# A SwiGLU down projection as seven block products over 1024 tokens

## The chip, the cores and the metric

The kernel runs on one core of one Trainium2 chip. The metric is the device time of one execution in microseconds; before the change the median of three runs is 2809.4 us. All operands are fp32 in HBM, and the result is too.

## The reference

One layer of a decoder trunk over 2048 tokens of width 1024 (D_FF is 2816). The part that matters is the channel sub-layer at the end and the norm after it:

```python
h = h + g1 * mix
u = rmsnorm(h, norm2_w[l]) * (1.0 + sc2) + sh2
ff = (jax.nn.silu(u @ w_ffn_gate[l]) * (u @ w_ffn_up[l])) @ w_ffn_down[l]
h = h + g2 * ff
return rmsnorm(h, final_norm_w)
```

Ahead of it stand the adaLN vectors, one input projection, four HGRN2 heads, four differential attention heads and the output projection.

## The kernel before

**Precision.** TensorE multiplies in a rounded fp32 form. Each operand is therefore split into a high part (a cast on ScalarE, L114) and a low part (the operand less its high part, on VectorE, L115), and each product is three matmuls: high by high, low by high, high by low. A matmul here has 128 stationary columns and 512 moving ones.

**Stages.** In the profiled execution: adaLN and the input projection until about 400 us, attention and HGRN2 until 1131, output projection and second norm until 1420, gate and up for the later 1024 tokens until 1842, their down projection until about 2100, gate and up for the earlier 1024 tokens until 2552, their down projection to the end. The later tokens (s=1, blocks 3 and 2) come before the earlier (s=0, blocks 1 and 0); a block is 512 tokens.

**Gate and up** (`activations`, `seven`, L954 to L1030). For each of 11 values of p two feature blocks of 128 are computed for 1024 tokens. Each such product is a 2 by 2 block product by seven products in place of eight (Strassen's method, in the form with 15 sums). `combine` makes the sums of u2, the input, ahead (`x`, `y`, `w`, `t1` to `t4`, each a high and a low tile, L855 to L928); `seven` makes the sums of the weights (`s1` to `s4`, L967 to L971) in two tiles of the tag wsum. Its seven products have 12 matmuls each. `up` multiplies the two results and stores them to `act_d` (L1027), one store of 256 KB for each feature block and token block.

**Down projection** (`down`, L1048 to L1114), once for each block of 512 tokens. It runs over 22 feature blocks f. A step loads the activations of f (256 KB, into a `slot`) and the row block of `w_down` (512 KB, into a `wraw`), splits both (`sh`, `sl`, `wh`, `wl`, four buffers each) and issues 24 matmuls: four token tiles, two column halves, three products (L1079). All eight PSUM banks hold one block's result. The last steps are held back and issued token tile by token tile (2 steps for s=1, 4 for s=0), so that a tile's scaling can begin while the next is multiplied. At f == 8 gate, norm weight and residual `h_d` are loaded (L1063 to L1069). At the end each tile is scaled by `g2` (L1106), added to the residual (L1108, L1111), normed (L1089 to L1098) and stored (L1099).

**What sets the order.** The program is written in one order, and a list scheduler then orders the instructions of each engine's queue by its own model of their times. Each engine works through its queue in order. Loads stand in SP's queue, most stores in POOL's. Beside the down projections of s=1 run `make_u2` for the earlier tokens and the parts of `combine(0)` (`first`, `second` in block 2; `third`, `fourth` behind it), handed to `down` as `others` and taken one a step.

Of the kernel before, what the change touches and what calls it, by code (L numbers as in the profile page):

```python
# [14 lines left out]
ALU = mybir.AluOpType  # L15
# [26 lines left out]
NRAW, NW, NTMP = 3, 4, 8  # L42
# [6 lines left out]
def kernel(ctx: ExitStack, tc: tile.TileContext, io: dict, out: bass.AP):  # L49
# [61 lines left out]
    act_d = [[dram.tile([P, TB], F32, name=f"actd{b}_{f}") for f in range(NF)] for b in range(NTB)]  # L111
# [718 lines left out]
    pu7 = ctx.enter_context(tc.tile_pool(name="pu7", bufs=1))  # L830
    pt5 = ctx.enter_context(tc.tile_pool(name="pt5", bufs=1))
    later.close()
    ps = ctx.enter_context(tc.tile_pool(name="ps", bufs=1, side="right"))
# [16 lines left out]
    def combine(s):  # L850
# [20 lines left out]
        def first():  # L871
            for kk in range(4):
                x, z = load(kk, 0, 0), load(kk, 0, 1)
                put("x", kk, x)
                DVE.tensor_tensor(x, z, x, op=ALU.subtract)
                w = load(kk, 1, 1)
                DVE.tensor_tensor(x, w, x, op=ALU.subtract)
                put("t2", kk, x)
                DVE.tensor_tensor(w, w, z, op=ALU.subtract)
                put("t3", kk, w)  # L880
                yield

        def second():
            for kk in range(4):
                put("y", kk, load(kk, 1, 0))
# [3 lines left out]
                yield  # L889

        def third():
            for kk in range(4):
                put("w", kk, load(kk, 1, 1))
                yield

        def fourth():
            for kk in range(4):
                x, z = load(kk, 0, 0), load(kk, 0, 1)
                DVE.tensor_tensor(x, z, x, op=ALU.subtract)
                w, y = load(kk, 1, 1), load(kk, 1, 0)  # L900
                DVE.tensor_tensor(x, w, x, op=ALU.subtract)
                DVE.tensor_tensor(x, y, x, op=ALU.subtract)
                put("t4", kk, x)
                yield

        def together():

            kept = []
            for kk in range(4):
# [3 lines left out]
                t2 = ps.tile([P, TB], F32, name="t2", tag="sh", bufs=4)  # L913
# [16 lines left out]
        return made, first(), second(), third(), fourth(), together()  # L930

    def big(name, tag, bufs, dt=F32):
        return (ps if tag == "wsum" else pf).tile([P, D], dt, name=name, tag=tag, bufs=bufs)
# [11 lines left out]
    def split_small(src):  # L945
        h = ps.tile([P, TB], F32R, name="sh", tag="sh", bufs=4)
        lo = ps.tile([P, TB], F32R, name="sl", tag="sl", bufs=4)
# [6 lines left out]
    def seven(src, f0, u, finish):  # L954
# [4 lines left out]
            load_big(src[:, (f0 + j) * P:(f0 + j + 1) * P].rearrange("(k p) c -> p k c", p=P), NK)  # L959
            for j in range(2)  # L960
# [51 lines left out]

    def activations(s, u):

        for p in range(NP):
# [7 lines left out]

            def up(j, t, ps, sb):
                a = sl[j, t]
                DVE.tensor_tensor(a, sb if ps is None else ps, a, op=ALU.mult)  # L1026
                POOL.dma_start(out=act_d[2 * s + t][2 * p + j], in_=a)  # L1027

            seven(w_gate, 2 * p, u, gate)
            seven(w_up, 2 * p, u, up)  # L1030

    def single(take):

        left = []

        def one():
            if not left:
                left.extend(take())
            return left.pop(0)
        return one  # L1040

    def down_step(b, f, at):

        t = at()
        SP.dma_start(out=t, in_=act_d[b][f])
        return f, split_small(t), split_big(load_big(w_down[f * P:(f + 1) * P, None, :], 1))

    def down(b, at, first, others=(), after=()):  # L1048
# [4 lines left out]
        tags = (("acc", 2), ("acc", 2), ("sc", 2), ("sc", 2), ("hg", 2), ("hg", 2), ("pv", 1), ("tr", 1))  # L1053
        pds = [bank(*t) for t in tags]
        place = slots([f"u{z}{k}" for z in "hl" for k in range(4)])
        ho = [place() for tt in range(NT)]
        place = slots(T4[4:])
        fw, g2 = place(), place()
        ws = []
        for f in range(NF):  # L1060
            ws.append(first.pop(0) if first else down_step(b, f, at))
            next(others, None)
            if f == 8:  # L1063
                for c in range(2):
                    cs = slice(c * TB, (c + 1) * TB)
                    SP.dma_start(out=g2[c], in_=gate_d[1][:, cs])
                    SP.dma_start(out=fw[c], in_=bcast_row(io["final_norm_w"][cs]))
                    for tt in range(NT):
                        SP.dma_start(out=ho[tt][c], in_=h_d[b][tt * P:(tt + 1) * P, cs])  # L1069

            if NF - (LAST if b else LAST0) <= f < NF - 1:
                continue
            for tt in range(NT):
                tsl = slice(tt * P, (tt + 1) * P)
                for cc in ((0,), (1,)) if not b and f == NF - 1 else ((0, 1),):
                    for g, a, w in ws:
                        for m, (x, y) in enumerate(((0, 0), (0, 1), (1, 0))):
                            for c in cc:
                                PE.matmul(  # L1079
                                    pds[2 * tt + c], a[x][:, tsl], w[y][:, c * TB:(c + 1) * TB],  # L1080
# [105 lines left out]
```

## Time and profile before

| | |
|---|---|
| median of 3 runs | 2809.4 us (2808.2 to 2815.19) |
| the profiled execution | 2806.66 us |
| its span | 2804.8 us |
| mean granted TensorE clock | 0.988 of full speed |
| TensorE busy | 2706.7 us, 97% |
| VectorE busy | 1709.4 us, 61% |
| ScalarE busy | 1124.3 us, 40% |
| GpSimd busy | 327.4 us, 12% |
| moved over the span | 403.52 MB, 144 GB/s |

Times of engines are busy times of one profiled execution. They overlap, so they don't add up to the span. TensorE's matmuls are pipelined, with ends that are modelled: a busy TensorE may still be waiting inside. The span runs from the first to the last instruction that the profile shows; the time of the execution is a little longer. In the rows, PE is TensorE, PEld its weight loads, DVE VectorE, ACT ScalarE, POOL GpSimd, SP SyncE, and L1079 is line 1079 of the kernel before.

### The profile page before, as it was taken

To read this page: it belongs to the slowest core of one execution; us is meant where nothing else is said; L and a number is where in the kernel's file an instruction comes from. 1 tells how busy PE (TensorE), PEld (TensorE's weight loads), DVE (VectorE), ACT (ScalarE), POOL (GpSimd) and SP (SyncE) were. 2 spreads that over 40 slices of the span, in tenths; PEclk is the share of its full clock that TensorE was granted. 3 is DMA by queue.
4 is the path that set the end of the run, shared out by engine and by line. 5 is a ranking of instruction groups with operands and counts; after the bars stand their busy time and mean duration, and the time that the engine had idled before them with its cause. 6 is when DMAs were issued, how large, how long until landed. Compare 5 with 4: busy or idle time off the path is not lost.

```text
span 2804.8 us, 40363 instructions
## 1 busy us (share of the span) xinstructions
PE 2706.7 (97%) x15017; PEld 2320.0 (83%) x15017; DVE 1709.4 (61%) x3456; ACT 1124.3 (40%) x2062; POOL 327.4 (12%) x493
## 2 busy tenths in 40 slices
PE   6999999999999998898999999999999999999998
PEld 5888879999999997897878888878887888888886
DVE  6434557777777779664585555553757555554354
ACT  4542135565565666543342222242433222222232
POOL 2552200000010000112210000020101000000010
PEclk9999999999999999998999999999999999999999
DMA  8765672434234220656542222274845222226461
GB/s 274 262 210 171 215 224 79 136 121 132 80 117 143 72 91 31 220 178 224 171 129 89 76 75 83 83 281 150 299 132 162 86 75 79 79 83 221 140 217 61
DMA packets 306104, 403.52 MB, mean 144 GB/s; under 512 B 22970, under 2 KB 208620, under 8 KB 305780
## 3 DMA queue, kind: packets, MB, share of 16 engines
q1 hardware_dynamic: 276788, 307.60, 34.4%
q0 software_dynamic: 29120, 93.35, 9.0%
q8 instruction: 118, 1.93, 0.3%
q14 instruction: 78, 0.64, 0.1%
HBM read 309.63 MB, written 91.23 MB: 143 GB/s over the span
## 4 chain that ended last, share of the span: by engine, by line
PE 74%; DMA 4%; DVE 4%; issue 3%; ACT 1%; POOL 1%; SPq 0%; POOLq 0%; DVEq 0%; ACTq 0%
PE ps_sc L985 8%; PE ps_hg L985 8%; PE ps_acc L985 8%; PE ps_acc L174 8%; PE ps_acc L162 5%; PE ps_acc L1079 4%; PE ps_sc L1079 4%; PE ps_hg L1079 4%; PE ps_pv L633 4%; PE ps_pv L1079 2%; PE ps_tr L985 2%; PE ps_pv L985 2%; PE ps_tr L1079 2%; PE ps_tr L629 2%; PE ps_sc L603 2%
## 5 line engine op out<-in xcount | busy, mean ns | idle before, releaser
L115 DVE TENSOR_TENSOR wl<-wraw,wh 128x1024 fp32r<-128x1024 f32 x252 | 307.5, 1221 | 98.4 <-ACT wh L114 94.9
L114 ACT CAST wh<-wraw 128x1024 fp32r<-128x1024 f32 x252 | 263.6, 1047 | 221.3 <-PE ps_acc L174 111.5
L174 PE MATMUL ps_acc<-wh,uh 128*128 128x256 f32 x1040 | 295.5, 286 | 0.8 <-ACT uh L505 0.6
L174 PE MATMUL ps_acc<-wl,uh 128*128 128x256 f32 x1040 | 293.8, 284 | 2.1 <-DVE wl L115 2.1
L174 PE MATMUL ps_acc<-wh,ul 128*128 128x256 f32 x1040 | 292.3, 284 | 0.0
L114 ACT CAST wh<-wsum 128x1024 fp32r<-128x1024 f32 x88 | 92.3, 1049 | 307.5 <-issue 142.7
L174 PEld LDWEIGHTS ps_acc<-wl,uh 128*128 128x128 f32 x1040 | 196.0, 189 | 4.9 <-DVE wl L115 2.3
L174 PEld LDWEIGHTS ps_acc<-wh,uh 128*128 128x128 f32 x1040 | 195.7, 189 | 3.8 <-ACT uh L505 1.4
L174 PEld LDWEIGHTS ps_acc<-wh,ul 128*128 128x128 f32 x1040 | 194.9, 189 | 2.3 <-issue 0.2
L115 DVE TENSOR_TENSOR sl<-slot,sh 128x512 fp32r<-128x512 f32 x88 | 60.5, 690 | 203.3 <-ACT sh L114 200.0
L612 ACT ACTIVATE s<-s,mx 128x2048 f32<-128x2048 f32 (+15 forms) x128 | 154.0, 1203 | 47.0 <-DVE mx L607 45.3
L607 DVE CUSTOM_DVE_ANT_0 s<-ps_sc,dist,mx 128x512 f32<-128x512 f32 x192 | 143.5, 748 | 44.1 <-PE ps_sc L604 39.6
L114 ACT CAST sh<-slot 128x512 fp32r<-128x512 f32 x88 | 54.2, 620 | 259.2 <-PE ps_tr L1079 217.5
L633 PE MATMUL ps_pv<-vt,wt 128*128 128x128 f32 x1088 | 150.8, 278 | 3.3 <-ACT wt L631 3.1
L633 PEld LDWEIGHTS ps_pv<-vt,wt 128*128 128x128 f32 x1088 | 140.4, 194 | 11.0 <-ACT wt L631 5.9
L115 DVE TENSOR_TENSOR wl<-wsum,wh 128x1024 fp32r<-128x1024 f32 x88 | 107.5, 1222 | 68.7 <-ACT wh L114 65.7
L162 PE MATMUL ps_acc<-ul,wh 128*128 128x512 f32 x352 | 141.9, 404 | 1.0 <-DMA ul<-ud 1.0
L162 PE MATMUL ps_acc<-uh,wh 128*128 128x512 f32 x352 | 142.1, 406 | 0.0
L1027 POOL DMA_DIRECT2D actd<-t x88 | 47.9, 544 | 798.1 <-DVE t L1026 793.8
L162 PE MATMUL ps_acc<-uh,wl 128*128 128x512 f32 x352 | 140.3, 400 | 0.4 <-DVE wl L115 0.4
L985 PE MATMUL ps_hg<-cuh,wh 128*128 128x512 f32 x352 | 139.6, 397 | 0.0
L985 PE MATMUL ps_hg<-cul,wh 128*128 128x512 f32 x352 | 139.5, 396 | 0.0
(406 smaller groups left out, 7028.1 us busy)
## 6 DMA issues: line engine op xcount, KB each, us to landing
wraw<-in_w_in_dram SPq DMA_DIRECT2D x88, 512.0 KB, 4.2
wraw<-in_w_ffn_down_dram SPq DMA_DIRECT2D x88, 512.0 KB, 3.7
wraw<-in_w_ffn_gate_dram SPq DMA_DIRECT2D x44, 512.0 KB, 3.9
wraw<-in_w_ffn_up_dram SPq DMA_DIRECT2D x44, 512.0 KB
actd<-t POOLq DMA_DIRECT2D x88, 256.0 KB, 2.5
slot<-actd SPq DMA_DIRECT2D x88, 256.0 KB, 5.0
ada_w<-in_w_ada_dram SPq DMA_DIRECT2D x64, 256.0 KB, 3.9
wraw<-in_w_out_dram SPq DMA_DIRECT2D x32, 512.0 KB, 4.2
```

Of the source, the lines that this page charges most:

```text
L114: ACT.copy(dst_h, src)
L115: DVE.tensor_tensor(dst_l, src, dst_h.bitcast(F32), op=ALU.subtract)
L162: PE.matmul(pa, a[:, k % 4, j * P:(j + 1) * P], c, start=n == 0, stop=n == 3 * NK - 1)
L174: PE.matmul(pa[:, j], a[:, tt * P:(tt + 1) * P], c[:, k % 4], start=n == 0, stop=n == 3 * NK - 1)
L603: PE.matmul(ps[:, :n], qs[m][0][:, qc], ks[m][pc][:, :n], start=True, stop=False)
L607: DVE.tensor_tensor_reduce(out=s[:, lo:hi], in0=ps[:, :hi - lo], in1=dist[:, u0_:u0_ + hi - lo], op0=ALU.add, op1=ALU.min, scale=-slope, s ...
L612: ACT.activation(s[:, :W], s[:, :W], AF.Exp, scale=-1.0, bias=mx[:, npiece - 1:npiece], accum_out=mx[:, 4:5])
L629: PE.transpose(out=pt[:, j - g], in_=S[0][:, j * P:(j + 1) * P], identity=ident)
L633: PE.matmul(pv[:, :P], wt[:, j - g], vq[j // 4][:, j % 4], start=j == 0, stop=j == i)
L985: PE.matmul(pa[:, cs], a, c[:, cs], start=first and i == 0, stop=i == 11 and cs.stop == TB, skip_group_check=not first)
L1027: POOL.dma_start(out=act_d[2 * s + t][2 * p + j], in_=a)
L1079: PE.matmul(pds[2 * tt + c], a[x][:, tsl], w[y][:, c * TB:(c + 1) * TB], start=g == 0 and m == 0, stop=g == NF - 1 and m == 2,)
```

## The change

The down projection, too, is made by seven products. `down(s)` now covers 1024 tokens at once: two token blocks by two halves of D_FF against two halves of D_FF by two halves of the columns. Each of the seven products runs over 11 values of k; a step has 12 matmuls (four token tiles, three products, 512 columns), and there are 77 steps for each s. Products 0 to 6 use two sets of four PSUM banks in turn; products 2 and 6 add to what the product before left in their set (`start` stays false).

- `activations` now makes feature blocks p and p + 11 in one group. `up` makes the four operand sums (L1050 to L1060) as the results come and stores seven tensors where it stored four (L1036).
- `weights(k)` makes the four sums of `w_down`'s blocks (L1017 to L1020), in the first of the two gate and up stages alone, between gate and up of each group, and stores them to `wd_d`.
- `down_load` loads two steps in a pair: two raw tiles of the tag wraw2 (NRAW is now 4), each filled by two loads of 256 KB, and each split as one tile of 128x1024 into `wh2` and `wl2` (four buffers, thus two pairs).
- `finished` combines a product's result when it is complete: `c2` and `c3` hold the shared partial results, `result` scales by `g2` (L1120) and adds to the residual (L1122). `g2` is now in one of the two wsum buffers, `fw` in g1's tile; the residual of all eight token tiles is loaded at step 11.
- `combine` has the parts `most` (taken every second step, from the ninth on, within `down(1)`) and `rest` (behind it); `first` to `fourth` go. The norms of s=1 come behind its down projection, those of the later half of s=0 at the start of product 6.

```diff
-NRAW, NW, NTMP = 3, 4, 8
+NRAW, NW, NTMP = 4, 4, 8
...
-        lo = ps.tile([P, TB], F32R, name="sl", tag="sl", bufs=4)
+        lo = ss.tile([P, TB], F32R, name="sl", tag="sh", bufs=4)
...
+    def weights(k):
+
+        r1, r2 = (load_big(w_down[f * P:(f + 1) * P, None, :], 1) for f in (k, k + NP))
+        b11, b12 = r1[:, :TB], r1[:, TB:]
+        b21, b22 = r2[:, :TB], r2[:, TB:]
+        DVE.tensor_tensor(b22, b22, b12, op=ALU.subtract)
+        DVE.tensor_tensor(b12, b12, b11, op=ALU.subtract)
+        DVE.tensor_tensor(b11, b22, b11, op=ALU.add)
+        DVE.tensor_tensor(b21, b11, b21, op=ALU.subtract)
+        for n, t in ((1, b11), (3, b22), (4, b12), (5, b21)):
+            POOL.dma_start(out=wd_d[n][k], in_=t)
...
+                elif (j, t) == (0, 1):
+                    s1, s2 = other(), other()
+                    DVE.tensor_tensor(s1, a, sl[1, 1], op=ALU.add)
+                    store(4, s1)
+                    DVE.tensor_tensor(s2, s1, sl[0, 0], op=ALU.subtract)
+                    store(1, s2)
+                    DVE.tensor_tensor(a, sl[0, 0], a, op=ALU.subtract)
+                    store(3, a)
+                    sl["s2"] = s2
...
+            fs = (p, p + NP)
+            seven(w_gate, fs, u, gate)
+            if s:
+                weights(p)
+            seven(w_up, fs, u, up)
...
+                SP.dma_start(out=raw[:, z * TB:(z + 1) * TB], in_=src)
+            if i + 1 < NS:
+                ops.append(split_big(raw))
...
+        def finished(n, tt):
+
+            pa = sets[n % 2][tt]
+            if n == 0:
+                ACT.copy(c2[tt], pa)
+            elif n == 1:
+                DVE.tensor_tensor(c2[tt], c2[tt], pa, op=ALU.add)
+            elif n == 2:
+                result(0, 0, tt, pa)
+            elif n == 3:
+                DVE.tensor_tensor(c3[tt], c2[tt], pa, op=ALU.add)
+            elif n == 4:
+                result(1, 1, tt, pa, ALU.add, c3[tt])
+
+                DVE.tensor_tensor(c2[tt], c2[tt], g2[:, TB:], op=ALU.mult)
+                DVE.tensor_tensor(ho[0][tt][1], ho[0][tt][1], c2[tt], op=ALU.add)
+            elif n == 5:
+                result(1, 0, tt, pa, ALU.subtract, c3[tt])
+            else:
+                result(0, 1, tt, pa)
...
+                for g, (a, w) in held:
+                    kk = g % NP
+                    for m, (x, y) in enumerate(((0, 0), (0, 1), (1, 0))):
+                        PE.matmul(
+                            sets[n % 2][tt], a[x][:, tt * P:(tt + 1) * P], w[y],
+                            start=kk == 0 and m == 0 and n not in (2, 6), stop=kk == NP - 1 and m == 2,
+                            skip_group_check=n in (2, 6),
+                        )
+                if k == NP - 1:
+                    finished(n, tt)
...
+    steps = down_load(1, 0) + down_load(1, 2)
+    _, norms = down(1, steps, itertools.chain([None] * 8, most))
+    run(calls(*norms), rest)
     activations(0, made)
+    steps = down_load(0, 0) + down_load(0, 2)
+    down(0, steps)
```

Lines in the rows that follow are those of each kernel's own text. L1079 is the old down projection's matmul and L1189 the new one's; L115 and L123 are the subtraction of a split.

**First place: the middle of a down projection.** TensorE's queue before, most of one step of 24 matmuls (`sh`, `sl` the activations, `wh`, `wl` the weights):

```order
L1079 MATMUL ps_acc<-wh_19347,sh 128x512 x2
L1079 MATMUL ps_acc<-wl_19348,sh 128x512 x2
L1079 MATMUL ps_acc<-wh_19347,sl 128x512 x2
L1079 MATMUL ps_sc<-wh_19347,sh 128x512 x2
L1079 MATMUL ps_sc<-wl_19348,sh 128x512 x2
L1079 MATMUL ps_sc<-wh_19347,sl 128x512 x2
L1079 MATMUL ps_hg<-wh_19347,sh 128x512 x2
L1079 MATMUL ps_hg<-wl_19348,sh 128x512 x2
L1079 MATMUL ps_hg<-wh_19347,sl 128x512 x2
```

TensorE's queue now, the first step of a pair (the first operand named is the weights' part, the second the activations'):

```order
L1189 MATMUL ps_hg<-wh_20071,wh_20064 128x512 x2
L1189 MATMUL ps_pv<-wh_20071,wh_20064 128x512
L1189 MATMUL ps_tr<-wh_20071,wh_20064 128x512
L1189 MATMUL ps_hg<-wl_20072,wh_20064 128x512
L1189 MATMUL ps_hg<-wh_20071,wl_20065 128x512
L1189 MATMUL ps_hg<-wl_20072,wh_20064 128x512
L1189 MATMUL ps_hg<-wh_20071,wl_20065 128x512
L1189 MATMUL ps_pv<-wl_20072,wh_20064 128x512
L1189 MATMUL ps_pv<-wh_20071,wl_20065 128x512
L1189 MATMUL ps_tr<-wl_20072,wh_20064 128x512
L1189 MATMUL ps_tr<-wh_20071,wl_20065 128x512
```

VectorE's queue now, at the end of product 2 (`t` a temporary, `g` the gate, `slot` the residual):

```order
L123 TENSOR_TENSOR wl_20011<-wraw_20007,wh_20010 128x1024
L123 TENSOR_TENSOR wl_20018<-wraw_20014,wh_20017 128x1024
L1120 TENSOR_TENSOR t_19963<-ps_acc,g_19252 128x512
L1120 TENSOR_TENSOR t_19969<-ps_acc,g_19252 128x512
L1120 TENSOR_TENSOR t_19975<-ps_sc,g_19252 128x512
L1120 TENSOR_TENSOR t_19981<-ps_sc,g_19252 128x512
L1122 TENSOR_TENSOR slot<-slot,t_19963 128x512
L1122 TENSOR_TENSOR slot<-slot,t_19969 128x512
L1122 TENSOR_TENSOR slot<-slot,t_19975 128x512
L1122 TENSOR_TENSOR slot<-slot,t_19981 128x512
L123 TENSOR_TENSOR wl_20065<-wraw_20061,wh_20064 128x1024
L123 TENSOR_TENSOR wl_20072<-wraw_20068,wh_20071 128x1024
```

On TensorE the four high by high matmuls of a pair's first step have moved to the front. On VectorE eight passes of `result` stand between one pair's two subtractions and the next pair's. Where `most` runs beside the loop, ten passes of `combine` stand in one row ahead of a pair's first subtraction, and three between it and the second.

**Second place: the handover from the down projection of s=1 to the next gate and up stage.** VectorE's queue before (`wsum` the sums of the first groups' weights):

```order
L115 TENSOR_TENSOR wl_20656<-wraw_20653,wh_20655 128x1024
L971 TENSOR_TENSOR wsum<-wraw_20867,wsum 128x512
L115 TENSOR_TENSOR sl<-wraw_20869,sh 128x512
L115 TENSOR_TENSOR wl_20872<-wraw_20867,wh_20871 128x1024
L115 TENSOR_TENSOR sl<-wraw_20998,sh 128x512
L115 TENSOR_TENSOR wl_20880<-wsum,wh_20879 128x1024
L1106 TENSOR_TENSOR t_20707<-ps_acc,slot 128x512
L967 TENSOR_TENSOR wsum<-wraw_20998 128x512
L1106 TENSOR_TENSOR t_20708<-ps_acc,slot 128x512
L1111 TENSOR_TENSOR slot<-slot,t_20707 128x512
L968 TENSOR_TENSOR wsum<-wsum,wraw_20996 128x512
L1111 TENSOR_TENSOR slot<-slot,t_20708 128x512
```

VectorE's queue now, from the first scaling of product 6 on:

```order
L1120 TENSOR_TENSOR t_20887<-ps_acc,g_19252 128x512
L1120 TENSOR_TENSOR t_20896<-ps_acc,g_19252 128x512
L123 TENSOR_TENSOR wl_21094<-wsum,wh_21093 128x1024
L1120 TENSOR_TENSOR t_20905<-ps_sc,g_19252 128x512
L123 TENSOR_TENSOR sl<-wraw_21212,sh 128x512
L1120 TENSOR_TENSOR t_20914<-ps_sc,g_19252 128x512
L1122 TENSOR_TENSOR slot<-slot,t_20887 128x512
L1122 TENSOR_TENSOR slot<-slot,t_20896 128x512
L1122 TENSOR_TENSOR slot<-slot,t_20905 128x512
L901 TENSOR_TENSOR t_21021<-t_21023,t_21021 128x512
L1122 TENSOR_TENSOR slot<-slot,t_20914 128x512
L969 TENSOR_TENSOR wsum<-wraw_21081,wraw_21083 128x512
```

The sums of the first group's weights stood ahead of the last scalings (the last of them, L971, five rows above the first L1106); now two of the four, L969 and L970, stand behind eleven rows that begin with product 6's scaling.

**Third place: the end.** VectorE's queue before, the last rows of the program:

```order
L1106 TENSOR_TENSOR t_25519<-ps_pv,slot 128x512
L1108 TENSOR_TENSOR slot<-slot,t_25519 128x512
L1094 TENSOR_TENSOR f_r<-fss 128x1
L1095 TENSOR_SCALAR f_r<-f_r 128x1
L1098 SCALAR_TENSOR_TENSOR slot<-slot,f_r 128x512 x2
L1106 TENSOR_TENSOR t_25520<-ps_tr,slot 128x512
L1108 TENSOR_TENSOR slot<-slot,t_25520 128x512
L1094 TENSOR_TENSOR f_r<-fss 128x1
L1095 TENSOR_SCALAR f_r<-f_r 128x1
L1098 SCALAR_TENSOR_TENSOR slot<-slot,f_r 128x512 x2
```

VectorE's queue now, from the last product's first scaling on (an L1131 for each lot, an L1132 and a second row of four L1136 follow):

```order
L1120 TENSOR_TENSOR t_25664<-ps_acc,g_24123 128x512
L1120 TENSOR_TENSOR t_25692<-ps_acc,g_24123 128x512
L1122 TENSOR_TENSOR slot<-slot,t_25664 128x512
L1120 TENSOR_TENSOR t_25720<-ps_sc,g_24123 128x512
L1120 TENSOR_TENSOR t_25748<-ps_sc,g_24123 128x512
L1122 TENSOR_TENSOR slot<-slot,t_25692 128x512
L1122 TENSOR_TENSOR slot<-slot,t_25720 128x512
L1131 TENSOR_TENSOR f_r<-fss 128x1
L1122 TENSOR_TENSOR slot<-slot,t_25748 128x512
L1131 TENSOR_TENSOR f_r<-fss 128x1
L1132 TENSOR_SCALAR f_r<-f_r 128x1 x2
L1136 SCALAR_TENSOR_TENSOR slot<-slot,f_r,fw 128x512 x4
```

Before, one token tile's row (L1098, two of them) stood behind the last column half. Now the scalings of four token tiles and the two rows of L1136 for them stand behind the last product.

## Rows read from the trace of the kernel before

**Rows 1.** The page's head: the span, and each engine's busy time, share and instructions.

```profile
span 2804.8 us, 40363 instructions
...
PE 2706.7 (97%) x15017; PEld 2320.0 (83%) x15017; DVE 1709.4 (61%) x3456; ACT 1124.3 (40%) x2062; POOL 327.4 (12%) x493
```

**Rows 2.** The page's chain that ended last: shares of the span by engine.

```profile
PE 74%; DMA 4%; DVE 4%; issue 3%; ACT 1%; POOL 1%; SPq 0%; POOLq 0%; DVEq 0%; ACTq 0%
```

**Rows 3.** Busy time by stretch: PE, PEld, DVE, ACT, POOL, PEclk, DMA share, GB/s.

```profile
1420.00:1842.00 422.00, 420.54 (x1810) 338.57 (x1811) 247.43 (x338) 124.78 (x174) 24.32 (x45) 0.99 0.28 89
1852.00:2092.00 240.00, 238.54 (x1048) 193.47 (x1047) 129.78 (x182) 89.16 (x133) 21.34 (x33) 0.99 0.62 213
2092.00:2140.00 48.00, 43.74 (x179) 33.49 (x177) 39.97 (x68) 17.39 (x33) 9.64 (x12) 0.96 0.65 208
...
2566.00:2792.00 226.00, 224.86 (x968) 181.97 (x966) 99.93 (x133) 68.75 (x104) 10.15 (x15) 1.00 0.44 143
```

**Rows 4.** The chain in order of time: start, us, twelve matmuls of a step.

```profile
2785.27 2.80 PE ps_pv L1079 x12
```

**Rows 5.** Groups by line, 1842 to 2092: busy us, mean ns; idle before, releasers.

```profile
L115 DVE TENSOR_TENSOR wl<-wraw,wh 128x1024 fp32r<-128x1024 f32 x43 | 52.6, 1223 | 9.3 <-ACT wh L114 9.2
L114 ACT CAST wh<-wraw 128x1024 fp32r<-128x1024 f32 x43 | 45.0, 1046 | 3.3 <-DMA wraw<-in_w_ffn_down_dram 3.3
L115 DVE TENSOR_TENSOR sl<-slot,sh 128x512 fp32r<-128x512 f32 x44 | 30.2, 689 | 80.1 <-ACT sh L114 76.9 <-PE ps_pv L1079 3.2
L114 ACT CAST sh<-slot 128x512 fp32r<-128x512 f32 x44 | 27.1, 619 | 108.5 <-PE ps_tr L1079 80.2 <-issue 24.7 <-PE ps_pv L1079 3.6
...
L199 DVE TENSOR_SCALAR slot<-slot,u_r 128x512 f32<-128x512 f32 x16 | 6.9, 480 | 1.2 <-POOL u_r L197 0.9 <-DMA slot<-actd 0.4
L535 DVE TENSOR_SCALAR t<-ps_pv,a,modc 128x512 f32<-128x512 f32 x8 | 6.5, 809 | 12.6 <-PE ps_pv L207 12.6
...
L1098 DVE SCALAR_TENSOR_TENSOR slot<-slot,f_r 128x512 f32<-128x512 f32 x8 | 5.6, 745 | 0.0
...
L1111 DVE TENSOR_TENSOR slot<-slot,t 128x512 f32<-128x512 f32 x8 | 5.3, 685 | 0.0
```

**Rows 6.** Timeline, middle of a down projection: start, us, instruction [idle before it].

```profile
1966.46 0.62 ACT L114 CAST sh<-slot 128x512 fp32r<-128x512 f32 x1 [4.02 <-PE ps_tr L1079]
...
1968.07 1.23 DVE L115 TENSOR_TENSOR wl<-wraw,wh 128x1024 fp32r<-128x1024 f32 x1 [0.25 <-ACT wh L114]
```

**Rows 7.** Timeline of a gate and up group: two of VectorE's passes.

```profile
1608.53 0.68 DVE L970 TENSOR_TENSOR wsum<-wraw,wraw 128x512 f32<-128x512 f32 x1
...
1609.13 0.68 DVE L971 TENSOR_TENSOR wsum<-wraw,wsum 128x512 f32<-128x512 f32 x1
```

**Rows 8.** DMA, 1990 to 2040, then 1852 to 2092: KB, us to landing.

```profile
DMA packets 7762, 17.70 MB, mean 354 GB/s; under 512 B 913, under 2 KB 913, under 8 KB 7758
...
slot<-hd SPq DMA_DIRECT2D x12, 256.0 KB, 7.6
```

**Rows 9.** TensorE's waits, 2088 to 2145: us, times, longest; a stretch as above.

```profile
PE ps_sc L985 <- DVE wl L115: 2.6, 1, 2.6
...
2132.00:2136.00 4.00, 3.82 (x13) 2.53 (x12) 3.84 (x7) 0.59 (x1) 0.00 (x0) 0.71 0.82 252
```

**Rows 10.** DMA, 1930 to 1980, 2600 to 2680 and 1420 to 1842, in turn.

```profile
t<-u2d SPq DMA_DIRECT2D x3, 256.0 KB, 3.4
...
out_dram<-slot POOLq DMA_DIRECT2D x4, 256.0 KB, 3.5
...
actd<-t POOLq DMA_DIRECT2D x41, 256.0 KB, 2.3
```

**Rows 11.** Timeline of the end: the last matmul and the scalings after it.

```profile
2790.46 0.40 PE L1079 MATMUL ps_tr<-wh,sl 128*128 128x512 f32 x1
...
2791.83 0.68 DVE L1106 TENSOR_TENSOR t<-ps_tr,slot 128x512 f32<-128x512 f32 x1
...
2795.17 1.42 DVE L1098 SCALAR_TENSOR_TENSOR slot<-slot,f_r 128x512 f32<-128x512 f32 x2 [0.73 <-POOL f_r L1096]
```

More of the change, by code (lines that the diff above doesn't have):

```diff
@@ L869, in load, with most @@
             return t
-        def first():
+        def most():
             for kk in range(4):
@@ L928, in together @@
                 yield
-        return made, first(), second(), third(), fourth(), together()
+        return made, together(), most(), rest()
     def big(name, tag, bufs, dt=F32):
-        return (ps if tag == "wsum" else pf).tile([P, D], dt, name=name, tag=tag, bufs=bufs)
+        return (ss if tag == "wsum" else pf).tile([P, D], dt, name=name, tag=tag, bufs=bufs)
     def load_big(src, k):
@@ L1022, in gate, with store, other @@
                 sl[j, t] = sb
+            def store(n, t):
+                POOL.dma_start(out=act_d[s][n][p], in_=t)
+            def other():
+                return ss.tile([P, TB], F32, name="asum", tag="asum", bufs=4)
             def up(j, t, ps, sb):
@@ L1048, in down @@
-    def down(b, at, first, others=(), after=()):
-        others = iter(others)
[L1053 to L1080, printed above, removed]
-                                    start=g == 0 and m == 0, stop=g == NF - 1 and m == 2,
-                                )
-            ws = []
-        for _ in others:
-            pass
-        made = after() if after else None
-        def norm(tt):
-            ss = ps.tile([P, 2], F32, name="fss", tag="fss", bufs=4)
@@ new lines, in down, with rows, result, norm @@
+    def down(s, steps, others=(), after=None):
+        others = iter(others)
+        sets = [[bank("acc", 2), bank("acc", 2), bank("sc", 2), bank("sc", 2)],
+                [bank("hg", 2), bank("hg", 2), bank("pv", 1), bank("tr", 1)]]
+        place = slots([f"u{z}{k}" for z in "hl" for k in range(NK)])
+        ho = [[place() for tt in range(NT)] for t in range(2)]
+        c2, c3 = ([ss.tile([P, TB], F32, name="cs", tag=t, bufs=4) for tt in range(NT)] for t in ("sh", "asum"))
+        fw, g2 = (big(n, *t) for n, t in (("fw", ("g1", 1)), ("g2", ("wsum", 2))))
+        last = LAST if s else LAST0
+        def rows(t, tt):
+            r = (2 * s + t) * TB + tt * P
+            return slice(r, r + P)
+        def result(t, c, tt, src, op=None, acc=None):
+            x = temp()
+            if op is not None:
+                DVE.tensor_tensor(x, acc, src, op=op)
+                src = x
+            DVE.tensor_tensor(x, src, g2[:, c * TB:(c + 1) * TB], op=ALU.mult)
+            h = ho[t][tt][c]
+            DVE.tensor_tensor(h, h, x, op=ALU.add)
+        def norm(t, tt, queue):
+            h = ho[t][tt]
+            sq = ss.tile([P, 2], F32, name="fss", tag="fss", bufs=4)
@@ L1114, in down @@
-        return made, (lambda: [norm(tt) for tt in range(NT)]) if b else None
+                cs = slice(c * TB, (c + 1) * TB)
+                DVE.scalar_tensor_tensor(h[c], h[c], r, fw[:, cs], op0=ALU.mult, op1=ALU.mult)
+                queue.dma_start(out=out[0, rows(t, tt), cs], in_=h[c])
+        def finished(n, tt):
[14 more added lines that the diff above has]
+                result(1, 0, tt, pa, ALU.subtract, c3[tt])
+            else:
+                result(0, 1, tt, pa)
@@ L1116, in calls @@
+        for _ in others:
+            pass
+        return made, [lambda t=t, tt=tt: norm(t, tt, POOL) for t in (1, 0) for tt in range(NT)] if s else []
     def calls(*fs):
```

157 lines of the change are left out of this document (88 added, 69 removed).

## The prediction

> **What bounds the kernel now.** I read the page's head first [rows 1]: TensorE is busy 2706.7 of 2804.8 us (97%), VectorE 61%, ScalarE 40%. The chain of work agrees [rows 2]: 74% of it is TensorE, DMA and VectorE have 4% each. Then the stretches [rows 3]: in the gate and up stage of the later tokens (1420 to 1842) TensorE is busy 420.5 of 422 us, in the down projections that follow 238.5 of 240, in the last ones 224.9 of 226, and at the handover from a down projection to the next gate and up stage 43.7 of 48. So a matmul taken out of a down projection is time taken out, as long as what feeds the others keeps up. The price of one is not its busy 0.4 us, which overlaps with the next: 12 of 128x512 take 2.80 us in the chain, 0.2333 each [rows 4]. Last, what feeds them [rows 5, 6]: a step of 24 matmuls (5.60 us) wants two casts on ScalarE (1.05 and 0.62) and two subtractions on VectorE (1.22 and 0.69). In the middle of the stage ScalarE waits 4.0 us in each step for TensorE to let a buffer go: the feeding waits for TensorE, not the other way round.
>
> **The change, part by part.** The sum is made against the profiled execution, 2806.66 us (span 2804.8), which lies 2.7 under the median of the three runs, 2809.4.
>
> Products: before 4 blocks x 22 steps x 24 = 2112 matmuls, after 2 x 77 x 12 = 1848, of the same shape. 264 x 0.2333 = **61.6 us off** the path, the whole gain.
>
> Operand splits: each pair of steps of the new loop is again 24 matmuls or 5.60 us, but both operands are now full tiles: 2 x 1.05 on ScalarE, 2 x 1.22 = 2.45 on VectorE [rows 5]. TensorE hides them. But the lead shrinks. The old loop held four steps of each operand; the new one holds two pairs, so a pair's casts start only when the pair before the running one is through. From there the two casts and the second subtraction take 1.05 + 0.25 + 2.45, some 3.7 us [rows 5, 6], against 5.6. Cover 1.9 us, 2.8 with the four high-by-high matmuls that the new order puts first (4 x 0.2333 more).
>
> VectorE's other work meets that cover. Per 1024 tokens there are 14 passes over 128x512 for each of four token tiles, 56 x 0.685 = 38 us, coming at the ends of products; back to back they start 0.60 apart [rows 7]. After product 2 eight passes stand in one row in VectorE's queue ahead of the next pair's splits: they begin about 1.4 us before the last matmul of the product (the first token tile is through by then) and end some 3.5 after it, the two subtractions at 6.0 to 6.5; the second is wanted at 5.6 + 0.9. So such a block costs 0 to 1.5 us. During the first projection combine's work is also in the queue: ten passes (6 us) ahead of one pair's first subtraction, three more before its second; by the same count that pair is late by about 2 us. The loads of h_d, 16 in a row (4.2 MB, at the 354 GB/s that the busiest stretch moved [rows 8] 12 us), stand in SP's queue between the third and the fourth pair's; the fourth is wanted at 3 x 5.6 - 3.7 = 13 us, so 0 to 4 us late. I take **+7 us** for the first projection (bounds 0 and 20) and **+2** for the second (0 and 8), which has no u2 work beside it.
>
> Handover to the second gate and up stage: now 4.3 us of idle TensorE [rows 3], over half of it one wait for a subtraction [rows 9]. After: g2 sits in one of the two wsum buffers until product 6 is scaled, so L969 and L970 stand behind eleven VectorE entries (one subtraction of 1.22, one of 0.69, nine passes at 0.6 apart): they end 8 us after the last matmul, the cast of that sum at 9. TensorE has the products of x and t2 of the first group to do meanwhile, 24 matmuls or 5.6 us: 3.4 idle. Then the product of y adds into the bank that L993 copies; that copy stands on ScalarE behind three casts into buffers which must first be written out as results (scaled at 13 to 16 us, 3.5 to land [rows 10]), so it comes at 20 us, when TensorE has been through since 17: 3.5 more. Three more waits, estimated at 4 us together (the longest of now is 2.6 [rows 9]), make it 11 us, 7 over now; and 2 for matmuls slower after gaps: now too the 4 us behind the wait show a granted clock of 0.71 [rows 9], between its levels of 1.2 and 2.4 GHz. **+9** (bounds 0, as today, and 16, with a store that takes a crowded load's 7.6 us [rows 8], and a second such wait).
>
> Tail: now from the last matmul's end (2790.9) to the end of the span it is 13.9 us; the last scaling ends at 2796.6, 5.7 after the matmul, and 8.2 us go to the store and the end [rows 11]. Before, the last token tile alone was left by then. After, by the order of the built program, the last step's 12 matmuls come by themselves and finish all four token tiles within 1.0 us of each other. Behind them on VectorE: eight passes at 0.6 (done 3.8 after, since two tiles are ready a little earlier), sums and powers in two lots, eight scalings at 0.71 in two rows of four, done 11.7 after. 11.7 - 5.7 = **+6** (3, if the rows close up, and 10).
>
> Gate and up stages: in the second, four passes more for each of 11 groups; in the first eight (four for the weights), that is 5.5 us in the 39.2 us of a group (14 products x 12 x 0.2333). VectorE was busy 247.4 of 422 [rows 3], 23.0 of 39.2; it goes to 28.5. POOL's queue gets 198 stores for 88, 2.3 us each to land [rows 10]; only the later loads of the same tensors wait for them. The weights' sums stand in VectorE's queue between two groups' products. **+2** (0 and 10). The fourth raw buffer lets loads of w_out go earlier and reorders the output projection a little: **0** (-4 and +5). Entry to the down projections, with two pairs loaded instead of two steps: **+1** (0 and 4).
>
> Sum: -61.6 + 7 + 2 + 9 + 6 + 2 + 0 + 1 = -33.6; from the median 2775.8, taken as **2775 us**. The distances to the bounds, added in squares, are -13 and +19: 2762 to 2794.
>
> **The rivals.**
> A. *Two pairs are too short a lead for the loads.* A raw buffer comes round every second pair, 11.2 us: its landing, cast, subtraction (1.05 + 0.25 + 1.22) and about 0.5 behind its twin's, so landing + 3.0. At the quiet 3.4 us of a 256 KB load [rows 10] that is 6.4, at the crowded 7.6 [rows 8] 10.6, both inside. But 1 MB is asked for each 5.6 us, where the old loop asked 768 KB; if landing grows with that to 7.6 x 4/3 = 10.1, the round is 13.1 and each pair waits half the excess: 0.95 x 76 pairs = 72 us, and the time is 2847, slower than now. Loads decide from a landing of 8.2 us; the gain is gone at 0.45 us a pair (9.1). Against it: 1 MB in 5.6 us is 187 GB/s, and the queue moved 354 over 50 us with loads of 256 and 512 KB [rows 8]. Chance 0.08, half of it slower by over 0.3%.
> The Trainium skill, "DMA: Bandwidth & Descriptors", section "Measured (HBM→SBUF, 128 partitions, SWDGE, issued from GpSimd)", says to batch transfers to 1 MiB or more, and under "Anatomy of one DMA — SWDGE (gpsimd) path" gives about 2.0 us fixed plus the bytes at 436 GB/s. If loads of 256 KB ran one after another, that would be an estimate of 4 x 2.6 = 10.4 us a pair, 4.8 over its matmuls, some 360 us in all. The crowded stretch [rows 8] doesn't bear this out, as its loads overlap.
> B. *VectorE becomes the bound of the first projection.* Splits 93, passes 38, combine's 36 passes 25, make_u2 and scaling 26 (16 x 0.48, 8 x 0.81, 16 x 0.745 [rows 5]): 182 of 216 us. If waits in its queue cost 20 instead of 7 and the handover 13, the time is 2792. For: 84% busy in order. Against: the blocks are spread. Chance 0.18, still faster.
> C. *Nearly all is hidden*: the handover as now, stalls of 2, tail as counted: 2809.4 - 61.6 + 8 = 2756. For: today's handover hides most of the same work. Chance 0.10.
> That the 264 matmuls don't go is excluded: the built program has 1848 in the new loop.
>
> **How the numbers follow.** The forecast (2762 to 2788) has 0.62, B (2788 to 2796) 0.18, C 0.10, A 0.08, and 0.02 is for something else. The range takes the forecast and B and leaves out C and A: 2762 to 2796. Under 0.3% (8 us) a measurement can't tell from no change. Faster: 0.62 + 0.18 + 0.10 = 0.90; A and the rest: 0.05 the same, 0.05 slower.
>
> **What would show it.** Right: 1848 matmuls of the new line 0.233 apart; ScalarE's casts in the new loop still waiting for TensorE; TensorE's idle time in waits of 1 to 4 us at the handover, at the ends of products and near combine's work; 20 us from the last matmul to the end. Wrong: the same gap at every pair with casts that wait for a load (A); VectorE near 95% through the first projection (B); or a gate and up stage over 431 us (11 x 39.2), which would put a price on the sums that I count as nearly free.

## The result

The changed kernel takes 2743.37 us (median of 4 runs, 2739.28 to 2746.97), the kernel before beside it 2811.67 (4 runs). The ratio is 0.9757, 95% interval 0.9737 to 0.9777: 68 us faster, where I forecast 34 and gave a range whose lower end was 2762. Run once more beside the kernel before, it was 2745.98 against 2810.25, ratio 0.9764 (0.9746 to 0.9783).

The page's head and its chain, after [rows 1, 2]:

```profile
span 2745.2 us, 40572 instructions
...
PE 2636.0 (96%) x14753; PEld 2269.7 (83%) x14753; DVE 1827.7 (67%) x3608; ACT 1143.4 (42%) x2050; POOL 384.9 (14%) x603
...
PE 69%; issue 5%; DMA 5%; DVE 4%; POOL 1%; ACT 1%; SPq 0%; DVEq 0%; POOLq 0%; ACTq 0%
```

TensorE is busy 70.7 us less and VectorE 118 us more; the chain is still TensorE's. The profiled execution after took 2746.97 us, the slowest of its four, and the one before 2806.66, less than any of the four timed beside it: the spans of these two traces lie 59.6 us apart, and they are what the account below compares. The other 9 us of the medians' 68 it doesn't cover. (A second profile of the same changed kernel has a span of 2738.2; 6.5 of the 7.0 us between the two lie ahead of the first gate and up stage.) Each stretch ends at a matmul of its line in the timeline; at the entry to a down projection, one product of gate and up still runs behind that matmul, before and after. In us:

| stretch | before | after | difference |
|---|---|---|---|
| start to the first matmul of gate and up, s=1 | 1406.4 | 1407.1 | +0.7 |
| gate and up, s=1 | 436.3 | 439.3 | +3.1 |
| to the first of gate and up, s=0 (down, s=1) | 263.5 | 226.0 | -37.5 |
| gate and up, s=0, with the handover | 436.1 | 441.0 | +4.9 |
| to the last matmul (down, s=0) | 248.2 | 212.5 | -35.6 |
| to the end | 14.4 | 19.2 | +4.8 |

132 matmuls fewer at 0.2333 are 30.8 us in each down stage; both gave about 36. So they lost no more to stalls than before, and something more was gained. The stretches after [rows 3]:

```profile
1407.00:1846.00 439.00, 432.69 (x1858) 347.02 (x1857) 309.65 (x441) 131.67 (x184) 67.36 (x124) 0.99 0.50 164
1856.00:2072.00 216.00, 212.82 (x960) 174.62 (x959) 157.32 (x201) 100.32 (x129) 24.32 (x35) 1.00 0.75 247
2072.00:2120.00 48.00, 39.49 (x155) 29.71 (x154) 40.34 (x67) 20.34 (x37) 6.89 (x12) 0.93 0.60 185
...
2540.00:2726.00 186.00, 186.00 (x821) 153.90 (x821) 114.50 (x134) 73.89 (x89) 9.48 (x12) 1.00 0.59 190
```

In the second down loop TensorE is busy 186.0 of 186 us. VectorE is at 73% in the first (157.3 of 216). What feeds TensorE there, 1856 to 2072 [rows 5]:

```profile
L123 DVE TENSOR_TENSOR wl<-wraw,wh 128x1024 fp32r<-128x1024 f32 x74 | 88.5, 1220 | 45.7 <-ACT wh L122 45.7
L122 ACT CAST wh<-wraw 128x1024 fp32r<-128x1024 f32 x73 | 73.5, 1050 | 91.4 <-PE ps_tr L1189 37.6 <-PE ps_sc L1189 36.8 <-PE ps_pv L1189 6.1
```

As before, ScalarE's casts wait for TensorE and the subtractions for the casts. No load is among the three releasers that the row names; the casts' waits for loads are 6.3 us in three waits, all ahead of 1915. What was gained on top is the pace of the matmuls. The chain in order of time, some pieces in the gate and up stage (L984) and in the new down loop (L1189) [rows 4]:

```profile
1502.42 2.80 PE ps_sc L984 x12
...
2580.80 1.36 PE ps_sc L1189 x6
```

Twelve matmuls of 128x512 still take 2.80 us in the gate and up stage (0.2333 each); six in the new loop take 1.36, that is 0.2267 each, at a granted clock of 1.00 of 2.4 GHz in the steady part of both (1440 to 1835 and 2530 to 2726). From start to start the mean is 232.4 ns over the old down loop, 226.7 in the steady part of the new one, 233.3 in gate and up before and after. 1848 x 5.7 ns is 10.5 us that no term of mine held.

### The profile page after: what moved, and what is told of

It is laid out like the page before. It is cut to its first block, busy times and chain, and to the rows that moved or that the text cites. A ratio compares the mean times of both kernels' runs of the same rounds, so it can differ in the third digit from the quotient of the medians.

```text
span 2745.2 us, 40572 instructions
## 1 busy us (share of the span) xinstructions
PE 2636.0 (96%) x14753; PEld 2269.7 (83%) x14753; DVE 1827.7 (67%) x3608; ACT 1143.4 (42%) x2050; POOL 384.9 (14%) x603
## 4 chain that ended last, share of the span: by engine, by line
PE 69%; issue 5%; DMA 5%; DVE 4%; POOL 1%; ACT 1%; SPq 0%; DVEq 0%; POOLq 0%; ACTq 0%
PE ps_hg L984 9%; PE ps_sc L984 9%; PE ps_acc L984 9%; PE ps_acc L182 7%; PE ps_acc L170 6%; PE ps_pv L641 4%; PE ps_acc L1189 3%; PE ps_sc L1189 3%; PE ps_hg L1189 3%; PE ps_tr L984 2%; PE ps_pv L984 2%; PE ps_tr L637 2%; PE ps_sc L611 2%; PE ps_sc L612 2%; PE ps_hg L703 2%
## 5 line engine op out<-in xcount | busy, mean ns | idle before, releaser
L122 ACT CAST wh<-wraw 128x1024 fp32r<-128x1024 f32 (+1 forms) x320 | 327.2, 1044 | 602.5 <-PE ps_hg L984 195.1
L123 DVE TENSOR_TENSOR wl<-wraw,wh 128x1024 fp32r<-128x1024 f32 (+1 forms) x320 | 384.1, 1214 | 193.8 <-ACT wh L122 190.5
L984 PE MATMUL ps_hg<-cuh,wh 128*128 128x512 f32 x352 | 139.1, 396 | 1.6 <-ACT cuh L122 1.3
L984 PE MATMUL ps_hg<-cul,wh 128*128 128x512 f32 x352 | 139.3, 396 | 0.0
L984 PE MATMUL ps_hg<-cuh,wl 128*128 128x512 f32 x352 | 139.1, 395 | 0.0
L611 PE MATMUL ps_sc<-ks,q 128*128 128x512 f32 (+2 forms) x320 | 132.3, 417 | 5.7 <-DVE mx L615 3.7
L639 ACT COPY wt<-ps_tr 128x512 f32<-128x512 f32 (+3 forms) x160 | 83.0, 519 | 112.1 <-PE ps_tr L637 110.6
L123 DVE TENSOR_TENSOR wl<-wsum,wh 128x1024 fp32r<-128x1024 f32 x88 | 107.4, 1222 | 33.0 <-ACT wh L122 33.0
```

The lines of the kernel that those rows point to most:

```text
L122: ACT.copy(dst_h, src)
L123: DVE.tensor_tensor(dst_l, src, dst_h.bitcast(F32), op=ALU.subtract)
L611: PE.matmul(ps[:, :n], qs[m][0][:, qc], ks[m][pc][:, :n], start=True, stop=False)
L639: ACT.copy(wt[:, :ge - g], pt[:, :ge - g])
L984: PE.matmul(pa[:, cs], a, c[:, cs], start=first and i == 0, stop=i == 11 and cs.stop == TB, skip_group_check=not first)
```

## Experiments

**Where the pace comes from.** My first theory looked at the loop: the new order of matmuls, banks and loads. The second at places: before, the split activations (stationary) and the split weights (moving) lie at distances of 384 bytes over a multiple of 512 in each partition (the moving operand's address less the stationary one's, by the addresses in the built programs); after, both come from one ring of tiles of 4096 bytes, and the distance is a multiple of 512. In the gate and up stages it is 288, for one product in seven 160. Three kernels (e1, e2 and e3 below) move tiles by keeping a few bytes free, and nothing else; c0 is the changed kernel once more.

> The changed kernel once more, unchanged. Both theories: 2743 us (2739 to 2747), matmuls of the new down loop at 227 ns, those of the gate and up stages at 233.

It took 2745.98 us; 227.0 ns in the new loop, 233.3 in gate and up.

The kernel before, its small tiles moved by 128 bytes (e1):

```diff
         lo = ps.tile([P, TB], F32R, name="sl", tag="sl", bufs=4)
+        ps.tile([P, 32], F32, name="pad", tag="pad", bufs=1)
```

> The kernel before, with 128 bytes kept free in the pool of the small tiles, so that the split activations (the down projection's stationary operand) lie a multiple of 512 bytes from the split weights (the moving one); now 384 over a multiple. Nothing else is moved. Theory of places (the pace of a matmul depends on where its two operands lie to each other in a partition): the 2112 matmuls of the old down loop go from 232.4 to 227 ns, 11 to 12 us faster, 2800. Theory of the loop (the pace comes with the new order of matmuls, banks and loads): 232.4 ns and no change, 2811.

It took 2797.81 us, ratio to before 0.9951 (0.9936 to 0.9966), 12.4 us faster. A piece of its chain in the old loop, now L1080:

```profile
2655.53 2.72 PE ps_acc L1080 x12
```

2.72 us for twelve; the mean is 226.8 ns, and 2112 x 5.6 ns is 11.8 us. The order is the old one, and the pace is the new one: the theory of the loop is out.

The changed kernel, its operands moved apart (e2):

```diff
-        return (ss if tag == "wsum" else pf).tile([P, D], dt, name=name, tag=tag, bufs=bufs)
+        w = D + 8 if tag in ("wh2", "wl2") else D
+        return (ss if tag == "wsum" else pf).tile([P, w], dt, name=name, tag=tag, bufs=bufs)[:, :D]
```

> The changed kernel with the tiles of the split operands 32 bytes longer, so that their distances to each other are no longer multiples of 512 bytes, in the down loops and, differently from product to product, in the gate and up stages. Theory of places: the down loop's matmuls go from 227 to 232 or 233 ns, about 10 us slower, 2753; the products of the gate and up stages whose distance becomes a multiple of 512 (one in seven or so) go from 233 to 227 ns, which gives 3 us of it back. Theory of the loop: 227 ns in the down loops, 233 in the gate and up stages, 2743.

It took 2749.81 us, ratio 0.9781 (0.9766 to 0.9795) against 0.9764 of c0. The down loop went to 232.3 ns, as expected, and gate and up, where distances now change from product to product, to 232.3 as well. 1848 x 5.3 less 3700 x 1.0 is 6 us; 3.8 were measured, and the intervals of the two ratios overlap, so the pace shows it and the time alone would not. Six matmuls of its new loop in the chain:

```profile
2609.37 1.40 PE ps_hg L1190 x6
```

One part of the expectation missed: the gate and up products that came to a multiple of 512 here took 230.6 ns, the others 232.6. They stand between products at other distances; that this is why they stayed over 227 is not shown.

The changed kernel with the gate and up stages at multiples of 512 (e3):

```diff
         wh, wl = big("wh2", "wh2", NW, F32R), big("wl2", "wl2", NW, F32R)
+        pf.tile([P, 56], F32, name="pad", tag="pad", bufs=1)
         split(wh, wl, raw)
...
         lo = ss.tile([P, TB], F32R, name="sl", tag="sh", bufs=4)
+        ss.tile([P, 32], F32, name="pad", tag="pad2", bufs=1)
```

> The changed kernel with 224 bytes kept free beside the large tiles and 128 beside the small ones, so that weights and activations of the gate and up stages lie a multiple of 512 bytes apart, too. Theory of places: some 3700 matmuls there go from 233.4 to 227 ns, 24 us faster, about 2720. Theory of the loop: no change, 2743.

It took 2724.29 us, ratio 0.9688 (0.9671 to 0.9704): 21.7 us under c0. A piece of its chain in gate and up (L986):

```profile
1502.27 2.72 PE ps_acc L986 x12
```

Twelve take 2.72 in place of 2.80; the mean went from 233.3 to 227.1 ns. So where all products of a loop lie alike, the pace follows the distance of the two operands, in either loop. The place of one operand alone doesn't explain it: in gate and up the moving operand starts 256 bytes over a multiple of 512 in the slow kernel and in e3 alike, and a stationary operand at 480 over it is slow there and fast in e1's down loop.

Then two more: the last kernel with the input projection moved as well, and the kernel before with its small tiles moved by 384 bytes, for the step of the rule:

```diff
+    gap = early.enter_context(tc.tile_pool(name="gap", bufs=1, side="right"))
+    gap.tile([P, 56], F32, name="gap")
     pw = early.enter_context(tc.tile_pool(name="pw", bufs=2, side="right"))
```

> The kernel of the run with all gate and up products at a multiple of 512 bytes, and now the weights of the input projection too, by 224 bytes kept free beside their pool. 1536 matmuls of 512 columns there are at 233 ns and should go to 227, 9 to 10 us faster; 2304 matmuls of 256 columns come to the same distance, and the output projection's 1536 went from 118.2 to 119.5 ns with it, so 3 us slower there. Sum by the theory of places: 6 to 7 us faster than the 2724 of that run, 2717. If the pace in the first 400 us is set by loads or by VectorE: 2724.

2721.2 us, ratio 0.9672 (0.9656 to 0.9688): 3 us less where 6 to 7 were expected, and not clear of the last one's interval. Its 512-column matmuls went from 233.0 to 228.3 ns only, over all of them, and those of 256 columns from 118.3 to 119.9 in the first 400 us, as the output projection's had. So the rule is not the same for 256 columns, and none came out for them: in e2's output projection, with eight distances mixed, they took 116.8 to 119.7, 117.3 at a multiple of 512, and the 88 in gate and up went the other way in e3, from 117.9 to 116.2. By its median this is the fastest version that was run, 91 us under the kernel before.

```diff
         lo = ps.tile([P, TB], F32R, name="sl", tag="sl", bufs=4)
+        ps.tile([P, 96], F32, name="pad", tag="pad", bufs=1)
```

> The kernel before with 384 bytes kept free instead of 128, so that stationary and moving operand of the old down loop lie 256 bytes over a multiple of 512 apart. If a multiple of 256 is enough, its 2112 matmuls take 227 ns; if it has to be a multiple of 512, 232 to 234 ns.

The old loop's matmuls took 226.8 ns, and the one run 2795.95 us. Six of them in its chain:

```profile
2601.92 1.36 PE ps_sc L1080 x6
```

A multiple of 256 is enough, then; 384, a multiple of 128, was not. What the trace shows beside it is that the next stationary operand is loaded while the moving one streams: a load of 0.19 us starts 3 ns after each matmul, at either pace. Why the distance matters was not tried, nor whether the stationary operand in use or the one being loaded counts: in these steady loops the two lie alike.

**The cover of VectorE's blocks.** The new loop lost next to nothing at the ends of products, where most of my 7 and 2 us were. Sixteen more passes were put behind product 2 of each down projection:

```diff
             x = temp()
+            if op is None and (t, c) == (0, 0):
+                for _ in range(4):
+                    DVE.tensor_tensor(x, src, g2[:, c * TB:(c + 1) * TB], op=ALU.mult)
```

> The changed kernel with four more passes for each token tile at the end of product 2 (the scaling made five times, same value each time), 16 passes of 0.6 us in each of the two down projections. The trace of the changed kernel leaves 2.93 us between a pair's second subtraction and the matmul that needs it, 0.34 where eight passes stand ahead. By the new order ten passes stand ahead of the first pair's second subtraction and some six between the next pairs' (5.9 us against 5.44). Theory that VectorE's passes are hidden until this cover is used up, and count one for one from there: 0.9 and then some 0.4 a pair, 4 us in all, with gaps of TensorE of about that size, 2747. Theory that they are covered by far more: no gap, 2743. Theory behind my term of 7 us, that such blocks lie on the path: up to 19 us, 2762.

It took 2746.69 us, ratio 0.9773 (0.9759 to 0.9788): no difference from c0 that can be told from noise. 2747 was the forecast of the first theory, 2743 that of the second, so the time doesn't part them, and the trace has to. The timeline at product 2's end in the second down loop, first the changed kernel's (the eight passes end at 2611.97, the pair's two subtractions stand in one row, then the matmul that needs the second):

```profile
2609.48 2.49 DVE L1122 TENSOR_TENSOR slot<-slot,t 128x512 f32<-128x512 f32 x4
...
2611.88 2.35 DVE L123 TENSOR_TENSOR wl<-wraw,wh 128x1024 fp32r<-128x1024 f32 x2
...
2615.54 0.39 PE L1189 MATMUL ps_hg<-wl,wh 128*128 128x512 f32 x1
```

and with the passes added (second subtraction, the weight load behind it, its matmul):

```profile
2613.38 1.21 DVE L123 TENSOR_TENSOR wl<-wraw,wh 128x1024 fp32r<-128x1024 f32 x1
...
2614.64 0.19 PEld L1192 LDWEIGHTS ps_hg<-wl,wh 128*128 128x128 f32 x1 [0.20 <-DVE wl L123]
2614.71 0.44 PE L1192 MATMUL ps_hg<-wl,wh 128*128 128x512 f32 x1
```

Two more passes ahead moved the slack from 1.31 us (2614.23 to 2615.54) to 0.12, that is one for one. My expectation had put the 0.34 us of another product's end here; with 1.31 the count gives 0.11. No gap, since the scheduler put the rest of the sixteen behind the splits of the next pairs, within what their 2.93 us bear. So passes were free as long as the cover lasted; that they count one for one beyond it was not reached here. The order of the changed kernel spends the cover almost to the end, too: the tightest pair of its second loop, at the end of product 4:

```profile
2674.07 1.21 DVE L123 TENSOR_TENSOR wl<-wraw,wh 128x1024 fp32r<-128x1024 f32 x1
...
2675.34 0.19 PEld L1189 LDWEIGHTS ps_hg<-wl,wh 128*128 128x128 f32 x1 [0.22 <-DVE wl L123]
2675.38 0.46 PE L1189 MATMUL ps_hg<-wl,wh 128*128 128x512 f32 x1
```

Its second subtraction ends at 2675.28, 0.1 us ahead.

**The handover.** The wait for L969 and L970 was to be taken out by giving g2 a tile of its own, paid for with two of the eight temporaries; the second run has the six temporaries alone.

```diff
-NRAW, NW, NTMP = 4, 4, 8
+NRAW, NW, NTMP = 4, 4, 6
...
-        return (ss if tag == "wsum" else pf).tile([P, D], dt, name=name, tag=tag, bufs=bufs)
+        return (ss if tag in ("wsum", "g2") else pf).tile([P, D], dt, name=name, tag=tag, bufs=bufs)
...
-        fw, g2 = (big(n, *t) for n, t in (("fw", ("g1", 1)), ("g2", ("wsum", 2))))
+        fw, g2 = (big(n, *t) for n, t in (("fw", ("g1", 1)), ("g2", ("g2", 1))))
```

> The changed kernel with the gate g2 in a tile of its own in place of one of the two wsum buffers; two temporaries of eight pay for it. L969 and L970 then stand ahead of product 6's scaling. Theory that the handover's cost is this wait: the first gap of TensorE (4.4 us) goes, its others (the copy L993 behind casts that wait for stores, about 4 us) stay, 3 to 4.5 us faster than the kernel with six temporaries and g2 in wsum (the next run): 2740. Rival, that another wait at once takes its place: no difference.

> The changed kernel with six temporaries in place of eight and nothing else, to tell what that costs in the run before. Either theory: 2743 to 2746, at most 3 us slower.

2748.21 us (0.9776, 0.9761 to 0.9791) and 2751.48 (0.9792, 0.9777 to 0.9806): 3.3 apart, as expected in size, though the intervals overlap. TensorE's waits at the handover, first the changed kernel's, then with six temporaries (2068 to 2116), then with g2 on its own:

```profile
PE ps_sc L984 <- ACT wh L122: 4.2, 1, 4.2
PE ps_acc L984 <- ACT t L993: 1.9, 1, 1.9
PE ps_sc L984 <- DVE wl L123: 1.0, 1, 1.0
```

```profile
PE ps_acc L984 <- ACT t L993: 8.4, 1, 8.4
PE ps_sc L984 <- ACT wh L122: 4.1, 1, 4.1
```

```profile
PE ps_hg L984 <- ACT cuh L122: 13.6, 1, 13.6
PE ps_pv L984 <- ACT wh L122: 0.7, 1, 0.7
```

With g2 on its own the 4.1 us wait for the cast of the first group's sums is gone, but the waits come later, in one of 13.6 for a cast that itself waits, at its end, for the store `out_dram<-slot`. Gaps and slower matmuls together (counted as in the next section) are 12.7 us at the handover of the changed kernel, 19.8 with six temporaries and 17.3 with g2 on its own: 2.5 us less in these two traces. The second expectation missed: six temporaries took 5.5 us more than c0 (the intervals just touch), and by the trace the copy L993 then holds TensorE for 8.4 us in place of 1.9. Neither version beats the changed kernel.

**Rival A, the loads.** One raw buffer fewer.

```diff
-NRAW, NW, NTMP = 4, 4, 8
+NRAW, NW, NTMP = 3, 4, 8
```

> The changed kernel with three raw buffers in place of four, for my rival A (the lead too short for the loads). A buffer then comes round after a pair and a half, 8.2 us; by my count it needs the landing and 3.0 us. Theory that loads are far from deciding: landings of 2.7 to 4.2 us give 5.7 to 7.2, no change in the quiet part, some waits beside combine's loads: 2743 to 2748. Theory A, that the loads were near deciding: a wait in nearly every pair, over 0.5 us each, 2780 and more.

2761.09 us (0.9828, 0.9802 to 0.9854), 15 over c0 and between the two expectations. Its casts in the second down loop, 2530 to 2730:

```profile
L122 ACT CAST wh<-wraw 128x1024 fp32r<-128x1024 f32 x72 | 73.5, 1052 | 116.3 <-PE ps_tr L1189 56.7 <-PE ps_sc L1189 36.2 <-DMA wraw<-actd 9.9
```

Even now they wait mostly for TensorE, for loads 9.9 of 116.3 us (2.5 of 106.4 in the changed kernel, 2530 to 2720). This loop lost 2 us, not half a microsecond a pair. By its trace some 4 us more went at the entry to the first gate and up stage, and some 4 in the first down loop: the 10.5 us between this profile and the changed kernel's, not the 15 of the medians. The landings of the changed kernel with four buffers, 1856 to 2072 (us at the end) [rows 8, 10]:

```profile
wraw<-wdd SPq DMA_DIRECT2D x44, 256.0 KB, 3.9
wraw<-in_w_ffn_down_dram SPq DMA_DIRECT2D x27, 256.0 KB, 4.3
...
slot<-hd SPq DMA_DIRECT2D x6, 256.0 KB, 5.7
```

They are half of the 8.2 us from which my count let loads decide. (The row of the activations' loads, `wraw<-actd`, shows no time to landing.)

## Why the prediction was wrong

The range missed, and rival C, that nearly all is hidden, still gave 2756. Two steps failed, each by some 10 us: one price for every matmul of this shape, and the stalls. Either alone would have left the sum inside the range, at 2764; both together took it out.

The terms add up to -34.6, where the prediction writes -33.6; its 2775 fits the right sum. Against the traces' 59.6 that is 25 us short: 10.5 for the pace, 10.6 for stalls and entry, 4.2 for the handover and 1.2 for the tail, less 2.0 for what came out dearer (gate and up 1.1, the stretch ahead of it 0.7, products 0.2); 0.5 stay open. By the steps:

- *Products, -61.6*: right. 264 fewer at the old loop's 232.4 ns are 61.4.
- *The price of one, 0.2333, for the old and the new loop alike* ("1848, of the same shape"): the step that failed first. The shape is the same and the pace is not: -10.5 us, shown by e1, e2 and e3. I had the number 2.80 for twelve from one row, and no reason to ask whether a matmul of that shape has one pace; the two loops of before, at 232.4 and 233.3, gave little hint of it.
- *Stalls, +7 and +2, and entry, +1*: the second step that failed, "so such a block costs 0 to 1.5 us ... I take +7". Measured: gaps and slower starts (all that starts over 0.3 us apart, less 0.23 each) came to 6.6 us in the first down stage, its entry among them, against 7.3 before, and to 0.1 in the second loop. The two stages' -37.5 and -35.6 are 132 x 0.2324 and 924 x 0.0057, 35.9, within 1.6 us. The cover was right (2.8 counted, 2.93 measured), and the ten passes of combine did cost 1.35 us (2 counted). What failed is the end of product 2: it falls in mid-pair, the pair's second step is still to come, and the matmul that wants the second subtraction comes 8.0 us after the product's last has ended, not 6.5. The 0 to 4 us for the loads of `h_d` don't show: TensorE's waits name no load, and those for casts come to 1.3 us. And having found bounds that began at 0, I took a number in the middle, where the order spoke for 0.
- *Handover, +9*: the mechanism was right, the size off. The timeline from the last matmul of the down projection (2072.25) on, after:

```profile
2079.46 0.68 DVE L969 TENSOR_TENSOR wsum<-wraw,wraw 128x512 f32<-128x512 f32 x1
2080.06 0.68 DVE L970 TENSOR_TENSOR wsum<-wraw,wsum 128x512 f32<-128x512 f32 x1
...
2081.58 1.03 ACT L122 CAST wh<-wsum 128x1024 fp32r<-128x1024 f32 x1
...
2094.04 0.58 ACT L993 COPY t<-ps_acc 128x512 f32<-128x512 f32 x1
```

L970 ends at 2080.74, 8.5 us after it (8 counted), the cast follows at 2081.6 (9), the copy L993 at 2094.0, 21.8 after it (20). Counted as above, gaps and slower matmuls come to 12.7 us (13 counted). But I set against it the 4.3 us of idle TensorE of before, and with slower matmuls counted there too it is 7.9: +4.8, and the stage is 4.9 longer. The stretch has a granted clock of 0.93, against 0.96, between the levels of 1.2 and 2.4 GHz, after waits of 4.2 and 1.9 us.
- *Tail, +6*: +4.8. The end, after (last matmul, then two rows of four scalings) [rows 11]:

```profile
2726.02 0.39 PE L1189 MATMUL ps_sc<-wh,wl 128*128 128x512 f32 x1
...
2730.92 2.74 DVE L1136 SCALAR_TENSOR_TENSOR slot<-slot,f_r,fw 128x512 f32<-128x512 f32 x4 [0.62 <-POOL f_r L1133]
...
2734.72 2.74 DVE L1136 SCALAR_TENSOR_TENSOR slot<-slot,f_r,fw 128x512 f32<-128x512 f32 x4 [0.60 <-POOL f_r L1133]
```

The last scaling ends at 2737.46, 11.05 us after the last matmul's end (11.7 counted).
- *Gate and up, +2*: the sums are free. VectorE is busy 309.7 of 439 us, 27.6 per 39.2 (28.5 counted), and from 1440 to 1835 neither trace has a gap. The +3.1 is at the stage's entry, where the same count gives 11.2 us against 8.1; what makes it was not looked for. With its entry the stage takes 439.3 us, over the 431 that I had named as a sign of being wrong; but it took 436.3 before, so the sign was badly set.

The Trainium skill's rule to batch transfers to 1 MiB or more ("DMA: Bandwidth & Descriptors", "Measured (HBM→SBUF, 128 partitions, SWDGE, issued from GpSimd)") stood beside my estimate of 360 us lost if the loads of 256 KB ran one after another. The traces of this case say that they don't: the four of a pair, those with a time at 3.9 to 4.3 us each in the first loop, come within the pair's 5.4 us of matmuls, so they overlap.

Rival B is out, too: VectorE is at 73% in the first down stage (84% counted), and the 6.6 us are all that TensorE lost there.

## What to carry to other kernels

A price per matmul belongs to a loop and to the places of its operands, not to a shape: before a gain is counted in matmuls, look at the time from start to start in each loop, and try a few bytes of padding, which alone gave this kernel 22 us. Where work is hidden, count the slack to the instruction that needs it, in the order that the scheduler made, and if the count says zero, write zero. When a wait at a handover is priced, measure the old one in the same way, gaps and slower matmuls together.

## What the runs showed of the hardware

At a granted clock of 1.00, matmuls of 128x512 (4-byte operands) start 226.7 to 227.1 ns apart in loops where stationary and moving operand always lie a multiple of 256 bytes apart in the partition (distances 0 and 256 over a multiple of 512 were run), and 232.4 to 234.1 where they lie 384, 288 or 160 over it. The faster pace is not there at once: behind a gap, six to ten matmuls run at the slower one (ten at 2521.3 to 2523.7 in the changed kernel's trace), and products at a multiple of 512 between others that are not (e2, gate and up) took 230.6. For 256 columns no rule came out: 118.3 ns at a distance of 224 and 119.9 at 0 in the input projection, but 117.9 and 116.2 for the few in gate and up.
